# Masked rows in place of 64-row matmuls in attention, and a 16-step blocked scan in the state space layer

## The chip, the cores and the metric

The kernel runs on one core of a Trainium2 chip. The metric is the device time of one execution in microseconds (us). TensorE is PE in the profile, VectorE is DVE, ScalarE is ACT, GpSimd is POOL and SyncE is SP. The queues of SP, ACT and POOL issue the DMAs.

## The reference

Two layers run on a prompt and on eight samples that continue cached sequences. The even layer holds a retention part and a sparse attention with grouped queries: per query block there are compressed keys, selected blocks and a window. The odd layer is a diagonal state space model, and this is its core:

```python
def _s5(u, x0_re, x0_im, lam_re, lam_im, b_re, b_im, c_re, c_im, d, log_step):
    ug = u.reshape(B, L, S5_GROUPS, S5_GROUP)
    dt = jnp.exp(log_step)[:, None]
    mag = jnp.exp(lam_re * dt)
    ang = lam_im * dt
    ab_re, ab_im = mag * jnp.cos(ang), mag * jnp.sin(ang)
...
    bu_re = jnp.einsum('blgc,gpc->blgp', ug, bb_re)
    bu_im = jnp.einsum('blgc,gpc->blgp', ug, bb_im)
    bu_re = bu_re.at[:, 0].add(ab_re * x0_re - ab_im * x0_im)
    bu_im = bu_im.at[:, 0].add(ab_re * x0_im + ab_im * x0_re)
    _, _, xr, xi = lax.associative_scan(_complex_affine_combine, (a_re, a_im, bu_re, bu_im), axis=1)
    y = jnp.einsum('blgp,gcp->blgc', xr, c_re) - jnp.einsum('blgp,gcp->blgc', xi, c_im)
    y = y.reshape(B, L, E) + d * u
    return y, xr[:, -1], xi[:, -1]
```

The state follows x[n+1] = A x[n] + B u[n] with a diagonal complex A, for 64 groups of channels. After it come a gelu and a gated unit with two large matrices.

## The kernel before, in words

The program is written in order, as phases, and a scheduler then fixes one static order of instructions for each engine. Generators are woven: `weave` takes turns among several of them by their stated lengths, so the text of the kernel decides roughly which matmuls stand beside which others.

- Projections and retention (0 to 760 us) come first and are not touched.
- `attention` (783 to 2240) runs 32 units, each a pair of a key group and a query tile. A unit loads its keys (`KA`, `KB`) and queries (`QA`, `QB`). `QB` has 128 rows, the low halves of the split queries and then the high ones; `QA[br]` has the high half in its first 64 rows, and mask rows from 64 on. `scores1` (L1033) computes the compressed scores with two matmuls per head, one on 128 rows (L1039) and one on rows 0 to 63 (L1040). `maxima` (L1122) takes row maxima of the scores before the real pass; its matmuls (L1136) read `kmask` rows, 96 or 64. The loop from L1160 then does the scores (L1182, L1183) and the values (L1171). Projections of the output (L270 to L272) are woven in.
- `sweep_5` (2240 to 2534) normalises the rows and computes the input `u` of the state space layer (L1650 to L1652). Woven with it, `discretise` (L1432) and `tables` (L1333) make powers of A and three kinds of tables: inputs (`wst_s`), outputs (`ca_s`) and responses within a block (`kp_s`). They are written to DRAM.
- `state_space` (L1702) works on blocks of 8 steps. `states_in` multiplies the input tables with blocks of `u` (L1760), two neighbouring blocks being joined with `half`, a product with A to the 8th. `scan` walks 128 steps over all pairs, and 8 more for the samples. `outputs` adds three matmuls per group: the response of the block itself with `T8` (L1846), and the state through `ca` (L1847, L1848), where the second half of the blocks again takes a `half` product.
- A stream `G` of matmuls for the gate (`wz`, L270 to L272 from the end of sweep_5 on) is cut into three parts by `GQ` and woven with the states, the scan and the outputs. For each tile of 24 matmuls POOL does three operations on 128 x 512 elements (L241, L1686). `sweep_E` (2988 to 3584) is the gated unit.

`T8` has two buffers; a refill is eight DMAs, four on SP's queue and four on POOL's (L1826).

Of the kernel before, what the change touches and what calls it, by code (L numbers as in the profile page):

```python
# [18 lines left out]
NT = 16  # L19
# [14 lines left out]
GQ = (80, 220, 40)  # L34
# [86 lines left out]
class K:  # L121
    def __init__(self, tc, a, o, stack, dbg=None):
# [817 lines left out]
    def attention_setup(self, P_, tp):  # L940
# [41 lines left out]
        T.update(KA=KA, KB=KB, VP=VP, tri=tri, triT=triT, idr=idr, cm=cm, cv0=cv0, fk=fk, fa=fa, nd=nd, CKB=CKB, CV=CV, ctx={}, late=[], n_loop=[0], done=set())  # L982

    def attention(self, units, fill, last):
# [30 lines left out]
        def queries(u):  # L1015
# [12 lines left out]
            if t < 4:  # L1028
                nc.vector.memset(QA[0][64:96].bitcast(F32), 0.0)
            nc.vector.tensor_tensor(out=QB[0:64], in0=ps[0:64], in1=QB[0:64], op=OP.subtract)  # L1030
            return QA, QB

        def scores1(u, c):  # L1033
            t, gg = u % NT, u // NT
            QA, QB, CKB = c["QA"], c["QB"], T["CKB"][gg]
# [21 lines left out]
            if t >= 4:  # L1057
# [21 lines left out]
                nc.scalar.copy(out=QA[0][64:96], in_=pb[0:32, 0:1].to_broadcast([32, 4, 128]))  # L1079
# [259 lines left out]
    def tables_in(self, P_):  # L1339
        nc, a, ident, keep = self.nc, self.a, self.ident, self.tc.keep_in_program_order  # L1340
        cp, pp = P_("cpp", 1), P_("ppp", 2, space=PSUM)
        AP = cp.tile([128, 2, 9, 32], F32, name="AP")
# [35 lines left out]
        def inputs(gq):  # L1378

            ab = wk.tile([128, 2, 2, 8, 16], F32, name="ab")  # L1380
            cmul(gq, ab[:, 0], ab[:, 1], BB[0], BB[1], slice(7, None, -1), False)
            return ab

        def store_inputs(gq, ab):

            ps = pp.tile([128, 2, 2, 128], F32, name="pq")
            for j in range(2):
                for i in range(2):
                    nc.tensor.transpose(ps[:, j, i], ab[:, i, j].rearrange("x j c -> x (j c)"), ident)
            ws = wk.tile([128, 2, 2, 2, 64], F32, name="ws")  # L1390
            for j in range(2):
                nc.scalar.copy(out=ws[:, j].rearrange("x r i p -> x i r p"), in_=ps[:, j].rearrange("x i (r p) -> x i r p", r=2))
            nc.sync.dma_start(out=self.wst_s[gq], in_=ws.rearrange("x j r i p -> x (j r i p)"))

        def outputs(gq):

            ca = wk.tile([128, 2, 2, 8, 16], F32, name="ca")
            cmul(gq, ca[:, 0], ca[:, 1], C[0], C[1], slice(1, 9), True)
# [4 lines left out]
        def response(gq, ca):  # L1403

            kp = pp.tile([128, 512], F32, name="pq")[0:32, 0:256].rearrange("x (j n) -> x j n", j=2)
# [5 lines left out]
            kt = wk.tile([32, 2, 128], F32, name="kt")  # L1411
            for j in range(2):
# [7 lines left out]
            nc.scalar.copy(out=kt[:, :, 16:128], in_=kp[:, :, 16:128])  # L1420
            nc.sync.dma_start(out=self.kp_s[gq // 2][64 * (gq % 2):64 * (gq % 2) + 64].rearrange("(j x) n -> x j n", j=2), in_=kt)
# [13 lines left out]
    def discretise(self, P_, pp, AP, BB, C):  # L1435
# [25 lines left out]
        raw = cp.tile([128, 8, 2, 64], F32, name="craw")  # L1461
# [66 lines left out]
        t1, t2 = cp.tile([128, 4, 32], F32, name="pw1"), cp.tile([128, 4, 32], F32, name="pw2")  # L1528
        for m in (1, 2, 4):
            src = AP[:, :, 1:m + 1]  # L1530
            br, bi = [AP[:, i, m].unsqueeze(1).to_broadcast([128, m, 32]) for i in range(2)]
            V.tensor_tensor(out=t1[:, 0:m], in0=src[:, 0], in1=br, op=OP.mult)
            V.tensor_tensor(out=t2[:, 0:m], in0=src[:, 1], in1=bi, op=OP.mult)
            V.tensor_tensor(out=AP[:, 0, m + 1:2 * m + 1], in0=t1[:, 0:m], in1=t2[:, 0:m], op=OP.subtract)
            V.tensor_tensor(out=t1[:, 0:m], in0=src[:, 0], in1=bi, op=OP.mult)
# [449 lines left out]
```

## Time and profile before

| | us |
|---|---|
| median of 3 runs (3555.49 to 3573.8) | 3567.69 |
| the profiled execution | 3586.12 |
| its span | 3584.1 |
| PE, DVE, ACT, POOL busy in the span | 3268.0, 1801.5, 1065.8, 641.6 |
| attention, 783 to 2240 | 1457 |
| sweep_5's rows and the tables, 2285 to 2534.5 | 249.5 |
| states, scan, outputs | 80, 275.8, 97.7 |
| gated unit, 2988 to 3584.1 | 596.1 |

The windows were cut where the first and last instructions of a stage lie. A stage whose engine is busy nearly all the time has that engine as its limit; in the others the reader looks for what is waited for. A matmul's duration overlaps its neighbour's, so what it costs is read from the step between two starts. A matmul of 32-bit numbers that isn't marked as rounded is two records in the trace.

### The profile page before, as it was taken

The page shows a single profiled execution, that of the slowest core. Times are in us where ns is not written, and L with a number is a line of the kernel's source. Part 1 is how long each engine was busy: PE and PEld are TensorE (multiplying, and loading weights), DVE is VectorE, ACT ScalarE, POOL GpSimd, SP SyncE. Part 2 cuts the span into 40 slices and gives each one's busy share as a digit, 9 for nine tenths or more (in the row PEclk, how much of TensorE's full clock was granted, in tenths as well). Part 3 has the DMA queues.
Part 4 walks back from the last instruction along what each step waited for, and adds up shares of the span by engine and source line. Part 5 has one row for each costly group of instructions (what it writes and reads, how often), then busy time and mean ns, then how long its engine had stood idle before and what let it go on. Part 6 is the DMA issues. An engine that isn't in the chain of part 4 may idle for free. (4 is left out here: it accounts for less than half of the span.)

```text
span 3584.1 us, 47826 instructions
## 1 busy us (share of the span) xinstructions
PE 3268.0 (91%) x17425; PEld 2662.5 (74%) x17425; DVE 1801.5 (50%) x4911; ACT 1065.8 (30%) x2312; POOL 641.6 (18%) x729
## 2 busy tenths in 40 slices
PE   7999999979999999979999999799885077999999
PEld 5888778856777778867888888799564065888887
DVE  6455644434555554445545542553799995111222
ACT  4222211113343443433333332442342033111110
POOL 1212221221111110011110000332563062000000
PEclk9999999987898998979999999899998598999999
DMA  5333431133221121222111111554842067222342
GB/s 172 113 119 134 148 76 36 38 90 98 79 76 54 49 75 67 77 70 74 61 63 51 47 42 59 161 177 130 249 153 75 0 190 200 97 71 71 112 136 90
DMA packets 308532, 347.77 MB, mean 97 GB/s; under 512 B 134568, under 2 KB 225256, under 8 KB 306120
## 3 DMA queue, kind: packets, MB, share of 16 engines
q1 hardware_dynamic: 235480, 225.70, 21.5%
q10 hardware_dynamic: 68240, 78.04, 6.4%
q0 software_dynamic: 4576, 40.97, 3.2%
q8 instruction: 138, 2.26, 0.3%
q14 instruction: 98, 0.80, 0.1%
HBM read 231.13 MB, written 117.61 MB: 97 GB/s over the span
## 5 line engine op out<-in xcount | busy, mean ns | idle before, releaser
L1171 PEld LDWEIGHTS ot<-VP,pe 128*128 128x128 f32 x3296 | 446.9, 201 | 37.6 <-issue 9.4
L1171 PE MATMUL ot<-VP,pe 128*128 128x65 f32 x3296 | 438.4, 279 | 0.0
L1187 ACT ACTIVATE pe<-st 128x512 f32<-128x512 f32 x412 | 244.1, 597 | 423.4 <-PE st L1183 327.8
L270 PE MATMUL mm<-we_hi,hT_hi 128*128 128x512 f32 x768 | 304.9, 397 | 0.2 <-ACT hT_hi L226 0.2
L271 PE MATMUL mm<-we_lo,hT_hi 128*128 128x512 f32 x768 | 302.8, 394 | 0.0
L272 PE MATMUL mm<-we_hi,hT_lo 128*128 128x512 f32 x768 | 301.9, 393 | 0.0
L272 PE MATMUL mm<-wz_hi,hT_lo 128*128 128x512 f32 x384 | 155.8, 406 | 144.3 <-POOL hT_lo L241 144.3
L1142 DVE CUSTOM_DVE_ANT_0 tp<-tp,tri 128x256 f32<-128x256 f32 (+3 forms) x352 | 174.5, 504 | 119.3 <-PE tp L1136 110.2
L1136 PE MATMUL tp<-KA,QA 96*128 96x512 f32 (+6 forms) x576 | 209.8, 413 | 0.4 <-DVE mc L1138 0.3
L270 PE MATMUL mm<-we,hT_hi 128*128 128x512 f32 x512 | 201.9, 394 | 5.7 <-ACT hT_hi L240 5.4
L271 PE MATMUL mm<-we,hT_hi 128*128 128x512 f32 x512 | 200.4, 391 | 0.0
L272 PE MATMUL mm<-we,hT_lo 128*128 128x512 f32 x512 | 200.3, 392 | 0.0
L272 PEld LDWEIGHTS mm<-wz_hi,hT_lo 128*128 128x128 f32 x384 | 73.9, 192 | 165.0 <-POOL hT_lo L241 147.6
L1182 PE MATMUL st<-QB,KB 128*128 128x512 f32 x412 | 191.5, 467 | 1.7 <-ACT pe L1187 1.6
L1138 DVE TENSOR_REDUCE mc<-tp 128x1 f32<-128x512 f32 (+2 forms) x196 | 129.9, 672 | 101.1 <-PE tp L1136 99.8
L1157 POOL TENSOR_TENSOR QA<-pms,c_nd 4x512 fp32r<-4x512 f32 x64 | 67.1, 1048 | 620.3 <-ACT pms L1156 606.3
L1183 PE MATMUL st<-QA,KA 100*128 100x512 f32 (+1 forms) x412 | 175.0, 427 | 0.7 <-POOL QA L1157 0.7
L270 PEld LDWEIGHTS mm<-we_hi,hT_hi 128*128 128x128 f32 x768 | 144.7, 188 | 30.4 <-issue 1.0
L272 PEld LDWEIGHTS mm<-we_hi,hT_lo 128*128 128x128 f32 x768 | 144.6, 188 | 30.4 <-issue 0.7
L270 PE MATMUL mm<-wz_hi,hT_hi 128*128 128x512 f32 x384 | 160.4, 418 | 7.0 <-ACT hT_hi L240 7.0
L271 PEld LDWEIGHTS mm<-we_lo,hT_hi 128*128 128x128 f32 x768 | 144.8, 188 | 29.0 <-issue 0.7
L271 PE MATMUL mm<-wz_lo,hT_hi 128*128 128x512 f32 x384 | 157.6, 410 | 0.0
(541 smaller groups left out, 7153.5 us busy)
## 6 DMA issues: line engine op xcount, KB each, us to landing
xT_in<-xT_s SPq DMA_DIRECT2D x48, 512.0 KB
x_in<-x_prompt SPq DMA_DIRECT2D x32, 512.0 KB
xT_s<-xT ACTq DMA_DIRECT2D x32, 512.0 KB
x_in<-x_s SPq DMA_DIRECT2D x32, 512.0 KB
wraw<-w_in_even SPq DMA_DIRECT2D x24, 512.0 KB
qd<-q_s SPq DMA_DIRECT2D x64, 128.0 KB
o_in<-o_s SPq DMA_DIRECT2D x16, 512.0 KB
x_s<-x_in ACTq DMA_DIRECT2D x16, 512.0 KB
```

The source lines that it names most:

```text
L270: nc.tensor.matmul(out=ps[:, 0:n], lhsT=hi[:, k], rhs=whi[:, k], start=k == 0, stop=False)
L271: nc.tensor.matmul(out=ps[:, 0:n], lhsT=hi[:, k], rhs=wlo[:, k], start=False, stop=False)
L272: nc.tensor.matmul(out=ps[:, 0:n], lhsT=lo[:, k], rhs=whi[:, k], start=False, stop=k == 7)
L1136: nc.tensor.matmul(out=pv[:, h], lhsT=qa[0:kmask, h0 + h], rhs=KA[br][0:kmask, (k0 % nt[br]) * 128:(k0 % nt[br] + w) * 128], start=True, s ...
L1138: nc.vector.tensor_reduce(out=mc[:, h0:h0 + hw, i], in_=pv, axis=AX.X, op=OP.max)
L1142: nc.vector.tensor_tensor_reduce(out=pv[:, h], in0=pv[:, h], in1=tri[:, m0:m0 + w].rearrange("p a b -> p (a b)"), scale=1.0, scalar=-3e38, ...
L1157: nc.gpsimd.tensor_tensor(out=qa[r0:r0 + 4], in0=pms.unsqueeze(1).to_broadcast([4, 4, 128]), in1=T["nd"].unsqueeze(2).to_broadcast([4, 4, ...
L1171: nc.tensor.matmul(out=ot[:, h], lhsT=pe[:, 128 * h:128 * h + 128], rhs=VP[br][:, k % nt[br]], start=k == lo and h == 0, stop=k == u and h ...
L1182: nc.tensor.matmul(out=ps, lhsT=KB[br][:, kc], rhs=qb, start=True, stop=False)
L1183: nc.tensor.matmul(out=ps, lhsT=KA[br][0:r0 + 4, kc], rhs=qa[0:r0 + 4].rearrange("p h q -> p (h q)"), start=False, stop=k not in masked)
L1187: nc.scalar.activation(out=pe, in_=ps, func=AF.Exp, scale=0.125)
```

## The change

In attention, `scores1`'s second matmul reads all 128 rows of `QB` against `CKZ`, which holds the high halves of the keys in rows 64 to 127, where `QB` has the high halves of the queries, and zeros in rows 0 to 63. In `maxima` the masks are 96 and 68 rows, and rows 64 to 67 of `QA[1]` are set to zero by POOL for each unit.

In the state space layer the blocks have 16 steps. The tables hold 16 powers for inputs and 17 for A, `u` is stored so that neighbouring blocks lie side by side, and the states come from two accumulating matmuls instead of a product with A to the 8th. Blocks are scanned in eight chains at once: 15 steps over 64 x 8 elements, seven steps that carry the chains' ends over, and 15 corrections of 64 x 7 elements with powers of A. The outputs have a fourth matmul for the off-diagonal half of the block. `T8` now covers two pairs instead of four.

```diff
-GQ = (80, 220, 40)
+GQ = (95, 200, 45)
...
+            nc.gpsimd.memset(CKZ[gg][0:64].bitcast(F32), 0.0)
+            nc.scalar.copy(out=CKZ[gg][64:128], in_=ckd[64:128, gg])
...
+            nc.gpsimd.memset(QA[1][64:68].bitcast(F32), 0.0)
...
                 nc.tensor.matmul(out=ps[:, h, 0:n], lhsT=QB[:, h], rhs=CKB[:, 0:n], start=True, stop=False)
-                nc.tensor.matmul(out=ps[:, h, 0:n], lhsT=QA[0][0:64, h], rhs=CKB[0:64, 0:n], start=False, stop=True)
+                nc.tensor.matmul(out=ps[:, h, 0:n], lhsT=QB[:, h], rhs=CKZ[:, 0:n], start=False, stop=True)
...
-            kmask = 96 if br == 0 and u % NT >= 4 else 64
+            kmask = 96 if br == 0 else 68
...
-            sh = [128, 2, 8, 16]
+            sh = [128, 2, 16, 16]
...
-                    nc.tensor.matmul(out=kp[:, j, 16:128], lhsT=b2[i], rhs=ca[:, i, j, 0:7].rearrange("x k c -> x (k c)"), start=i == 0, stop=i == 1)
+                    nc.tensor.matmul(out=kp[:, j, 16:256], lhsT=b2[i], rhs=ca[:, i, j, 0:15].rearrange("x k c -> x (k c)"), start=i == 0, stop=i == 1)
...
-                        for r in range(2):
-                            nc.tensor.matmul(out=s[:, r, 0:264], lhsT=ws[:, gl % 2, r], rhs=UT[q][:, 2 * gl + r], start=True, stop=True)
...
+                            for r in range(2):
+                                U, o_ = UT[q][:, 4 * (gq % 4) + 2 * j + r], s[:, 2 * j + r]
+                                nc.tensor.matmul(out=o_[:, 0:136], lhsT=ws[:, 1, r], rhs=U[:, 0:136], start=True, stop=False)
+                                nc.tensor.matmul(out=o_[:, 0:128], lhsT=ws[:, 0, r], rhs=U[:, 136:264], start=False, stop=True)
...
+            def step(nx, cur, k, n):
+
+                w = yo.tile([128, 2, 64, 8], F32, name="scan", tag="y2")
+                m = [AT[:, k, i].unsqueeze(2).to_broadcast([128, 64, n]) for i in range(2)]
+                V.tensor_tensor(out=w[:, 0, :, 0:n], in0=cur, in1=m[0], op=OP.mult)
                 for i in range(2):
                     D, O = slice(64 * i, 64 * i + 64), slice(64 - 64 * i, 128 - 64 * i)
-                    V.tensor_tensor(out=w[1][O], in0=x[D], in1=m[1][D], op=OP.mult)
...
+                    V.tensor_tensor(out=w[O, 1, :, 0:n], in0=cur[D], in1=m[1][D], op=OP.mult)
+                for i in range(2):
+                    V.tensor_tensor(out=nx, in0=nx, in1=w[:, i, :, 0:n], op=OP.add)
+
+            def scan():
+
+                for j in range(1, 16):
+                    step(X[:, :, 16 + 8 * j:24 + 8 * j], X[:, :, 8 + 8 * j:16 + 8 * j], 1, 8)
+                    yield
+                for b in range(1, 8):
+                    step(X[:, :, 136 + b:137 + b], X[:, :, 135 + b:136 + b], 16, 1)
+                    yield
+                Y = X[:, :, 9:16]
...
+                for j in range(15):
+                    w = yo.tile([128, 2, 64, 8], F32, name="scan", tag="y2")
+                    for i, x in enumerate((Y, ys)):
+                        V.tensor_tensor(out=w[:, i, :, 0:7], in0=x, in1=AT[:, j + 1, i].unsqueeze(2).to_broadcast([128, 64, 7]), op=OP.mult)
+                    x = X[:, :, 17 + 8 * j:24 + 8 * j]
+                    for i in range(2):
+                        V.tensor_tensor(out=x, in0=x, in1=w[:, i, :, 0:7], op=OP.add)
                     yield
...
+                            T8 = T8s[gp // 2 % 2]
+                            for j in range(8):
+                                (nc.gpsimd if j % 2 else nc.sync).dma_start(out=T8[16 * j:16 * j + 16, :, 16 * j:256], in_=self.kp_s[gp // 2].rearrange("(g c) k -> c g k", c=16)[:, :, 0:256 - 16 * j])
...
-                            nc.tensor.matmul(out=y[:, r, 0:264], lhsT=T8[:, 2 * gl + r], rhs=U, start=True, stop=False)
-                            nc.tensor.matmul(out=y[:, r, 0:136], lhsT=ca[:, r, gl % 2], rhs=X[:, g, 0:136], start=False, stop=False)
-                            nc.tensor.matmul(out=y[:, r, 136:264], lhsT=ca[:, r, gl % 2], rhs=xh[:, r], start=False, stop=True)
...
+                            nc.tensor.matmul(out=y[:, r, 0:264], lhsT=T[:, 0:128], rhs=U, start=True, stop=False)
+                            nc.tensor.matmul(out=y[:, r, 0:128], lhsT=T[:, 128:256], rhs=U[:, 136:264], start=False, stop=False)
+                            nc.tensor.matmul(out=y[:, r, 128:264], lhsT=A[:, 0], rhs=X[:, g, 0:136], start=False, stop=False)
+                            nc.tensor.matmul(out=y[:, r, 0:128], lhsT=A[:, 1], rhs=X[:, g, 8:136], start=False, stop=True)
...
-            weave((scan(), 136), (self.take(G, b_), b_))
+            weave((scan(), 38), (self.take(G, b_), b_))
```

Three places show how the instructions stand. The first is PE in attention, at the end of one unit's compressed scores, before:

```order
L1039 MATMUL tp<-CKB_6687,QB 128x16
L1040 MATMUL tp<-CKB_6687,QA 128x16
L719 MATMUL tp<-c_ident,qn 128x64 x4
L729 MATMUL tp<-c_ident,kn 128x64
L1136 MATMUL tp<-KA_6659,QA 128x128 x2
```

and now (`CKZ` is the new tile, L1140 the line of the maxima):

```order
L1043 MATMUL tp<-CKB_6663,QB 128x16
L1044 MATMUL tp<-CKZ_6665,QB 128x16
L718 MATMUL tp<-c_ident,qn 128x64 x4
L728 MATMUL tp<-c_ident,kn 128x64
L1140 MATMUL tp<-KA_6635,QA 128x128 x2
```

Nothing moved here; the second matmul reads other tiles. The second place is DVE at the end of the scan before, where the first `half` products of the outputs (L1778) come in:

```order
L1789 TENSOR_TENSOR X<-X,scan 128x64
L1784 TENSOR_TENSOR scan<-X,AT_23296 128x64
L1787 TENSOR_TENSOR scan<-X,AT_23296 64x64 x2
L1788 TENSOR_TENSOR X<-X,scan 128x64
L1778 TENSOR_TENSOR h_25874<-X,AT_23296 64x256
L1789 TENSOR_TENSOR X<-X,scan 128x64
```

and DVE now, from the last step over eight chains to the first of the seven that carry their ends:

```order
L1789 TENSOR_TENSOR scan<-X,AT_23421 128x512
L1792 TENSOR_TENSOR scan<-X,AT_23421 64x512 x2
L1794 TENSOR_TENSOR X<-X,scan 128x64x8 x2
L1789 TENSOR_TENSOR scan<-X,AT_23421 128x64
L1792 TENSOR_TENSOR scan<-X,AT_23421 64x64 x2
L1794 TENSOR_TENSOR X<-X,scan 128x64 x2
```

A step still has five operations, of eight times the elements in the first 15. The third place is POOL in the outputs, with `T` the two buffers of `T8`, `yS` the samples' part of the result and `fin` the samples' final states, before:

```order
L1826 DMA T_0_23298<-kp_s_283 16x8x112
L1855 COPY yS<-y_26383 128x4x8
L1775 TENSOR_TENSOR h_26528<-X,AT_23296 128x256
L1813 COPY fin<-XS 128x64
L1775 TENSOR_TENSOR h_26548<-X,AT_23296 128x256
L1826 DMA T_0_23298<-kp_s_283 16x8x80
```

and now:

```order
L1855 DMA T_1_23424<-kp_s_254 16x4x176
L1855 DMA T_1_23424<-kp_s_254 16x4x144
L1859 DMA ca<-ca_s_238 128x2x256
L1855 DMA T_0_23423<-kp_s_255 16x4x240
L1879 COPY yS<-y_25574 128x4x8
L1855 DMA T_0_23423<-kp_s_255 16x4x208
```

The products are gone from POOL, and the refills of the two buffers of `T8` follow each other closely, with the copy of `yS` inside one of them.

## Rows read from the trace of the kernel before

**Rows 1.** The page: PE's busy tenths in 40 slices of 89.6 us.

```profile
PE   7999999979999999979999999799885077999999
```

**Rows 2.** Windows by stage: PE, PEld, DVE, ACT, POOL busy (records), clock, DMA share, GB/s.

```profile
783.00:2240.00 1457.00, 1410.02 (x8015) 1132.74 (x8015) 714.07 (x2433) 532.32 (x1223) 165.56 (x215) 0.91 0.22 68
...
2285.00:2534.50 249.50, 242.37 (x1993) 226.68 (x1991) 104.74 (x288) 95.58 (x219) 98.81 (x112) 0.99 0.57 164
2534.50:2614.50 80.00, 64.49 (x252) 46.43 (x253) 75.09 (x157) 24.95 (x57) 43.72 (x50) 0.98 0.72 227
2614.50:2742.00 127.50, 115.39 (x479) 91.32 (x477) 121.48 (x210) 62.62 (x118) 84.11 (x67) 0.96 0.43 137
2742.00:2890.30 148.30, 11.13 (x37) 8.01 (x37) 134.90 (x477) 3.60 (x7) 11.47 (x12) 0.55 0.02 7
2890.30:2988.00 97.70, 86.61 (x487) 73.69 (x487) 85.10 (x144) 39.20 (x70) 61.57 (x95) 0.97 0.83 240
```

**Rows 3.** Timeline of PE around a 64-row matmul: start us, duration us.

```profile
2122.43 0.40 PE L272 MATMUL acc<-wo_hi,hT_lo 128*128 128x512 f32 x1
2122.75 0.44 PE L1136 MATMUL tp<-KA,QA 64*128 64x384 f32 x1
2123.12 0.50 PE L270 MATMUL acc<-wo_hi,hT_hi 128*128 128x512 f32 x1
2123.46 0.39 PE L271 MATMUL acc<-wo_lo,hT_hi 128*128 128x512 f32 x1
```

**Rows 4.** Timeline of PE around a 96-row matmul.

```profile
2107.29 0.34 PE L1136 MATMUL tp<-KA,QA 96*128 96x384 f32 x1
2107.47 0.40 PE L1182 MATMUL st<-QB,KB 128*128 128x512 f32 x1
2107.70 0.40 PE L1183 MATMUL st<-QA,KA 100*128 100x512 f32 x1
```

**Rows 5.** Groups of weight loads in attention, 64-row maxima alone.

```profile
L1136 PEld LDWEIGHTS tp<-KA,QA 64*128 64x128 f32 x264 | 45.1, 199 | 46.5 <-issue 34.5 <-DVE mc L1142 3.7 <-DVE KB L1011 1.4
```

**Rows 6.** Timeline of PE in one unit's compressed scores.

```profile
1818.57 0.30 PE L1040 MATMUL tp<-CKB,QA 64*128 64x80 f32 x1
1818.80 0.30 PE L1039 MATMUL tp<-CKB,QB 128*128 128x80 f32 x1
```

**Rows 7.** Line L1171 in 1816 to 1818.4: durations ns, first and last start.

```profile
L1171 PEld LDWEIGHTS ot<-VP,pe x16: 189/192/192, 1816.5 to 1818.2; 128*128 128x128 f32 x16
L1171 PE MATMUL ot<-VP,pe x16: 220/275/275, 1816.7 to 1818.3; 128*128 128x65 f32 x16
```

**Rows 8.** Timeline of DVE in sweep_5.

```profile
2400.10 0.41 DVE L1369 TENSOR_TENSOR cm<-C,AP 128x256 f32<-128x256 f32 x1
2400.43 0.68 DVE L1615 TENSOR_TENSOR h_lo<-tp,h_hi 128x512 fp32r<-128x512 f32 x1
2401.03 0.41 DVE L1371 TENSOR_TENSOR cm<-C,AP 128x256 f32<-128x256 f32 x1
```

**Rows 9.** Timeline of DVE in the scan while POOL is idle.

```profile
2799.69 0.27 DVE L1784 TENSOR_TENSOR scan<-X,AT 128x64 f32<-128x64 f32 x1
2801.17 0.27 DVE L1784 TENSOR_TENSOR scan<-X,AT 128x64 f32<-128x64 f32 x1
```

**Rows 10.** Timeline of POOL and DVE in the scan beside the gate stream.

```profile
2640.34 1.29 POOL L241 TENSOR_TENSOR hT_lo<-xT_in,hT_hi 128x512 fp32r<-128x512 f32 x1
2640.50 1.28 DVE L1788 TENSOR_TENSOR X<-X,scan 128x64 f32<-128x64 f32 x1
```

**Rows 11.** Groups of DVE in the same stretch of the scan.

```profile
L1784 DVE TENSOR_TENSOR scan<-X,AT 128x64 f32<-128x64 f32 x40 | 24.2, 605 | 1.4
```

**Rows 12.** Timeline of PE in the outputs.

```profile
2944.16 0.38 PE L1848 MATMUL y<-s,ca 128*128 128x128 f32 x2
2944.38 0.61 PE L1846 MATMUL y<-UT,T 128*128 128x264 f32 x2
```

**Rows 13.** DMA issues in the outputs: KB each, median us to landing.

```profile
T<-kp_s POOLq DMA_DIRECT2D x6, 56.0 KB, 3.9
```

More of the change, by code (lines that the diff above doesn't have):

```diff
@@ L972, in attention_setup @@
         CKB = [cp.tile([128, 128], F32R, name=f"CKB{i}") for i in range(2)]
+        CKZ = [cp.tile([128, 128], F32R, name=f"CKZ{i}") for i in range(2)]
         cv = cp.tile([128, 2, 64], F32, name="CV")
@@ L1527, in discretise @@
         aim = tt(mag, sn, OP.mult, AP[:, 1, 1])
[L1528 to L1535, printed above, removed]
-            V.tensor_tensor(out=t2[:, 0:m], in0=src[:, 1], in1=br, op=OP.mult)
-            V.tensor_tensor(out=AP[:, 1, m + 1:2 * m + 1], in0=t1[:, 0:m], in1=t2[:, 0:m], op=OP.add)
-            yield
@@ L1544, in discretise @@
+        yield from doublings(AP)
+        BP = cp.tile([128, 2, 17, 32], F32, name="BP")
+        keep(V.tensor_copy(out=BP[:, :, 0], in_=AP[:, :, 8]))
+        V.tensor_copy(out=BP[:, :, 1], in_=AP[:, :, 16])
+        yield from doublings(BP)
+        for k in (0, 8, 16):
+            n = min(8, 17 - k)
+            AT = cp.tile([128, 8, 2, 32, 2], F32, name="AT", tag="cw")
             for r in range(2):
@@ L1557, in discretise @@
         fim = tt(tt(tt(aim, lre, OP.mult), tt(nr, lim, OP.mult), OP.subtract), den, OP.mult)
-        w1, w2 = [cp.tile([128, 32, 16], F32, name=f"bw{i}") for i in range(2)]
+        bw = cp.tile([128, 2, 32, 16], F32, name="bw", tag="cw")
+        w1, w2 = bw[:, 0], bw[:, 1]
         fr, fi = [f.unsqueeze(2).to_broadcast([128, 32, 16]) for f in (fre, fim)]
@@ L1750, in states_in @@
                     nc.tensor.transpose(ps[:, 0], raw, ident)
[L1751 removed]
+                    V.tensor_copy(out=UT[q][:, :, 128:136], in_=ps[:, 0].rearrange("x (b g) -> x g b", b=8))
                     yield
[L1753 to L1755 removed]
+                    for gq in range(4 * q, 4 * q + 4):
+                        s = pp.tile([128, 4, 256], F32, name="sp")
+                        for j in range(2):
@@ L1785, in step @@
                 for i in range(2):
                     D, O = slice(64 * i, 64 * i + 64), slice(64 - 64 * i, 128 - 64 * i)
-                    V.tensor_tensor(out=w[O, 1], in0=cur[D], in1=AT[D, j, 1], op=OP.mult)
-                V.tensor_tensor(out=nx, in0=nx, in1=w[:, 0], op=OP.add)
-                V.tensor_tensor(out=nx, in0=nx, in1=w[:, 1], op=OP.add)
-            def scan():
-                for n in range(128):
-                    step(X[:, :, n + 9], X[:, :, n + 8], 1)
+                    V.tensor_scalar(out=ys[O], in0=Y[D], scalar1=-1.0, scalar2=None, op0=OP.mult)
@@ L1794, in scan @@
+                for j in range(15):
[3 more added lines that the diff above has]
+                    x = X[:, :, 17 + 8 * j:24 + 8 * j]
+                    for i in range(2):
+                        V.tensor_tensor(out=x, in0=x, in1=w[:, i, :, 0:7], op=OP.add)
                     yield
-                for b in range(8):
-                    step(XS[:, :, b], X[:, :, b], 0)
-                    yield
+                step(XS, X[:, :, 0:8], 0, 8)
@@ L1823, in outputs @@
                 for q in range(8):
-                    T8 = T8s[q % 2]
-                    for j in range(8):
-                        (nc.gpsimd if j % 2 else nc.sync).dma_start(out=T8[16 * j:16 * j + 16, :, 16 * j:128], in_=self.kp_s[q].rearrange("(g c) k -> c g k", c=16)[:, :, 0:128 - 16 * j])
                     for gl in range(4):
@@ L1840, in outputs @@
-                        w = half(X[:, gs, 8:136], gs)
-                        for i in range(2):
-                            V.tensor_tensor(out=xh, in0=xh, in1=w[i], op=OP.add)
+                            T8 = T8s[gp // 2 % 2]
+                            for j in range(8):
+                                (nc.gpsimd if j % 2 else nc.sync).dma_start(out=T8[16 * j:16 * j + 16, :, 16 * j:256], in_=self.kp_s[gp // 2].rearrange("(g c) k -> c g k", c=16)[:, :, 0:256 - 16 * j])
+                            y2f = yo.tile([128, 4 * 264 + 8], F32, name="y2", tag="y2")
@@ new lines, in outputs @@
+                        yg = y2[:, 2 * (gl % 2):2 * (gl % 2) + 2]
+                        for r in range(2):
+                            o_ = 264 * (2 * (gl % 2) + r)
+                            yh, yi = [v.rearrange("p (h x) -> p h x", h=2)[:, :, 0:128] for v in (y2f[:, o_:o_ + 272], y[:, r, 0:272])]
+                            nc.scalar.activation(out=yh.rearrange("p h (b j) -> p h b j", j=16), in_=yi.rearrange("p h (j b) -> p h b j", b=8), func=AF.Gelu_apprx_tanh)
+                        nc.scalar.activation(out=yg[:, :, 128:136], in_=y[:, :, 128:136], func=AF.Gelu_apprx_tanh)
```

142 lines of the change are left out of this document (66 added, 76 removed).

## Prediction

> **What bounds the kernel now.** I read the 40 slices first: TensorE (PE) is full nearly everywhere, and the one hole, digits 8, 8 and 5 in slices 31 to 33, lies at about 2690 to 2960 us [rows 1]. Then the windows, one for each stage that the change touches [rows 2]. Attention (783 to 2240) has PE busy 1410 of 1457 us: the length of PE's stream is the length of the stage. So has sweep_5 (2285 to 2534.5), 242 of 249.5. In the states (to 2614.5) PE has 64 and VectorE (DVE) 75 of 80 us, so DVE sets the pace. The scan takes 276 us in two parts: 127.5 beside the gate stream, with DVE at 121, and 148 alone, where DVE runs 135 us and PE 11. The outputs (97.7 us) have PE at 87, DVE at 85 and the DMA engines at 0.83, all close together. So attention is to be judged by PE's stream, the scan by DVE's, and the outputs by three things at once.
>
> **Attention: row modes.** Around a lone 64-row matmul the starts are 2122.43, 2122.75, 2123.12, 2123.46: steps of 0.32, 0.37 and 0.34 us [rows 3]. Elsewhere a 512-column matmul on full rows takes a step of 0.23 us (2107.47 to 2107.70), and a 384-column one on 96 rows, between its neighbours on full rows, 0.18 [rows 4]. So the visit costs 0.09 before, 0.19 in itself and 0.11 after, 0.38 in all; 96 rows cost none of it. There are 264 such matmuls in the maxima [rows 5], in 188 unbroken stretches by the order. Neighbours share an entry and an exit, so I take the middle of 0.19 and 0.38, 0.285: 188 x 0.285 = 54 us (ends 36 and 71). With masks of 96 and 68 rows all of these go. In the compressed scores every second matmul has 64 rows; the step is 0.23 although only 80 columns pass [rows 6]. Where matmuls of 65 columns with a new weight each stand in a row on 128 rows, 16 take from 1816.7 to 1818.3, 0.107 each [rows 7]. 32 units x 8 matmuls x 0.123 = 31 us. Together 85 (67 to 102). As PE is idle for 47 us of the stage already, something else ends last at times, and a shorter stream will meet it more often: I take 72. For the unit POOL gets one small memset of 4 x 512 more; POOL is busy for 166 of 1457 us and that hides it; uncovered, 32 of them at the 1.29 us of a full 128 x 512 operation [rows 10] are 41 us at most. The granted clock is 0.91 here and 0.99 in sweep_5 [rows 2]; if half of that gap closed with a fuller stream, 4% of 1410, 56 us more would go, which I don't count. Term: **-72** (0 to -102).
>
> The Trainium skill ("TensorE: Matmul & The Clock Gate", Part 3, "What overlaps and what doesn't") says that weight loads overlap matmuls in flight only where their row groups differ. By that the new scores, all on 128 rows, would pay load and matmul in turn and gain nothing, and the term would be 31 smaller. The trace disagrees: the 16 loads of 192 ns stand beside matmuls that start every 107 ns on the same rows [rows 7].
>
> **Tables and sweep_5.** The tables hold 16 powers instead of 8. PE: 64 matmuls of 240 instead of 112 columns; 128 columns in two passes take 0.22 us, the step from 2944.16 to 2944.38 [rows 12], so 64 x 0.22 = 14; 64 more transposes of 128 columns in one pass, 0.11, are 7. The gate stream's split (95, 200, 45) brings 33 more of its matmuls ahead of the states by the order: 33 x 0.23 = 8. DVE: 192 operations of 512 instead of 256 elements, 0.60 against 0.33 between starts [rows 8], add 51 us to 105 busy of 249.5, so PE's stream covers them, if they come in time. By the order some 70 of the table matmuls now stand behind the last matmul of the rows' sweep, and there little else covers DVE. 14 + 7 + 8 = 29, less the 7 us that PE is idle there, plus some 3 of that tail, where the second set of powers on DVE falls too: **+25** (15 to 45).
>
> **States.** The half products (two DVE operations and one on POOL for each of 32 pairs), two additions and the spill go; two matmuls of 136 and 128 columns replace one of 264, at the same columns. PE's 64 us remain, and DVE has little left: 80 becomes 68, **-12** (-20 to +5, the upper end if the DMA share of 0.72 is what holds it).
>
> **Scan.** Before, 136 steps of five operations on 64 elements, 1.48 us each alone (2799.69 to 2801.17) [rows 9]. After, by the order: 15 steps of five on 512 elements, 7 of five on 64, 15 corrections of four on 448, and one more step that falls beside the outputs. An operation of 64 takes 0.27 and the next starts 0.03 later [rows 9]; one of 512 takes 0.68 [rows 8]. So 75 x 0.71 + 7 x 1.48 + 2 + 60 x 0.65 = 53 + 10 + 2 + 39 = 104.5 us of DVE's own. To that comes POOL. POOL's operation of 2640.34 lasts 1.29 us, and DVE's addition issued 0.16 later takes 1.28 instead of 0.27 [rows 10]: DVE stands still while POOL works. In this stretch 40 steps [rows 11] of 1.48 are 59 us, POOL is busy for 84, and 127.5 pass [rows 2]: 143 less an overlap of 15. The scan keeps 463 of the gate stream's 511 matmuls, so POOL has 84 x 463/511 = 76. 104.5 + 76 - 13 = 168 against 276: **-108**. Ends: no overlap, 181 (-95); no mutual stop at all, about 120, where PE's 463 x 0.23 = 107 and DVE's 104.5 are what is left (-156). I take the first since the row shows the stop on the same two engines and formats.
>
> The Trainium skill ("SBUF — State Buffer", "SBUF: two separate sides") calls it an exclusive lock on the port pair that DVE and GpSimd share, held for a whole instruction. It asks for a DVE operation with two SBUF inputs and a GpSimd operation that reads SBUF, which the wide scan operations and the gate stream still are; by it the stage comes to 168 to 181, and the trace agrees with the 1.28 us.
>
> **Outputs.** Per channel group one matmul of 128 columns more: 64 x 0.22 = 14 us of PE, and 15 more matmuls of the gate stream, 3.5. The half products and the reads of the spill go, so most of DVE's 85 us vanishes. The activation becomes three instructions instead of one, on ScalarE; its 39 busy us of 97.7 hide that, even if they all doubled. Tables are 6.5 instead of 2.4 MB, output coefficients 8.4 instead of 4.2, and 4.2 of spill go: 23.5 MB become 28. At 240 GB/s [rows 2] that is 117 us. T8 is refilled for each two pairs instead of four: four POOL issues, then 3.9 us to landing [rows 13], with a copy that waits for the activation between them. Two buffers make that some 7.3 us per step where 6.1 pass now (97.7/16): 117 us again. **+20** (0 to +35).
>
> **Sum.** -72 + 25 - 12 - 108 + 20 = -147. The profiled execution took 3586.1 us, its span 3584.1 and 2.0 around it; 3439 after. The median of the runs is 18.4 below the profiled one, so 3439 - 18 is about **3420** as a median.
>
> **The rivals.**
> 1. The row modes bring nothing: the waits on DVE, ScalarE and POOL in attention take the place of the visits. For it: PE's stream is woven so that many engines come due at once, and the 47 idle us. Against it: at 714 of 1457 us DVE is far from full. 72 less gain: 3492. 15%.
> 2. The wide operations aren't held up, because their time overlaps POOL's. For it: an overlap of 15 us is there already. Against it: [rows 10]. 48 more gain: 3372. 14%.
> 3. The tables' DVE work bounds sweep_5, since what was 105 us becomes 156 and stands in few places: 15 to 20 us over the term, about 3440 to 3460. 12%.
> 4. Slower than before: the T8 refill becomes a chain of last matmul, issue on POOL behind a waiting copy, landing, first matmul, with no two pairs in flight. It must eat 167 us (147 and the 20 already counted), so each of 16 steps must take 6.1 + 10.4 = 16.5 us; the parts give 2.2 of issue + 3.9 + 6.1 = 12.2 us even fully in turn, 3420 + 80 = 3500. Only if a POOL wait of 4 us comes to each would it tip; then 3570 or more. 3%, and 4% for 3500.
>
> **How the numbers follow.** The forecast has 52%, the rivals 15, 14, 12 and 7. I predict 3420; its own range is 3385 to 3455. The range for 8 in 10 takes in rivals 1 and 3 and most of 2: 3345 to 3495. 0.5% of the time, 18 us, is about what a measurement of this kernel can tell from no change; only rival 4's far end falls outside of faster: faster 0.95, same 0.02, slower 0.03.
>
> **What would show it.** After the change the windows should show: attention about 1385 us with no 64-row matmul and a 128-row step of 0.11 in the scores; states of 68 with DVE mostly idle; a scan of about 168, with wide DVE operations of 0.7 us alone and over 1.3 beside POOL; outputs of about 117 with DMA above 0.8. I am wrong if the attention window shrinks by under 40 us, if wide operations run at 0.7 beside POOL's, or if the outputs show PE waiting for T8's landing on each step.

## The result, and the profile after

The changed kernel takes 3412.47 us (median of 4 runs, 3401.74 to 3436.16), the one before 3561.59 in the same comparisons. The ratio is 0.9587, with a 95% interval of 0.9528 to 0.9646. The forecast was 3420, faster. The profiled execution took 3436.16 us with a span of 3434.4, 149.7 below the span before; by terms the forecast had 147. Both profiled executions lie 24 us above the median of their kernel, so the spans can be compared as well as the medians. The sum came out better than its terms did, as the windows show.

The first view is the page's slices of the changed kernel, to be read against [rows 1]. The hole has narrowed to slice 32, where PE falls to 4 tenths.

```profile
PE   7999999996999999988999998799898497999999
```

The next view is the windows of the changed kernel by stage, cut at the first and last instruction of each, with the columns of [rows 2]: attention, then the rows' sweep, the tail of the tables up to the first states' matmul, the states, the scan, the outputs and the gated unit.

```profile
785.40:2111.90 1326.50, 1275.83 (x7912) 1075.51 (x7912) 700.03 (x2378) 527.01 (x1218) 180.92 (x246) 0.94 0.23 73
...
2169.00:2428.90 259.90, 240.94 (x1934) 223.00 (x1934) 149.47 (x284) 94.18 (x218) 71.98 (x86) 0.96 0.55 160
2428.90:2483.70 54.80, 43.10 (x204) 27.52 (x203) 33.44 (x52) 19.73 (x45) 29.52 (x32) 0.88 0.81 240
2483.70:2554.10 70.40, 61.25 (x379) 53.09 (x378) 3.74 (x18) 22.91 (x42) 22.84 (x19) 0.98 0.84 254
2554.10:2724.50 170.40, 114.61 (x474) 90.53 (x473) 156.68 (x180) 61.02 (x115) 106.58 (x67) 0.83 0.30 103
2724.50:2837.50 113.00, 102.08 (x632) 88.66 (x630) 6.20 (x13) 41.98 (x128) 61.77 (x107) 1.00 0.85 245
2837.50:3434.40 596.90, 570.67 (x2554) 466.19 (x2552) 140.59 (x217) 86.96 (x153) 1.50 (x2) 0.98 0.33 104
```

Cut by the same marks, four stages of the kernel before (attention, rows' sweep, tail, scan):

```profile
782.70:2216.50 1433.80, 1387.90 (x7912) 1115.21 (x7912) 703.48 (x2378) 529.57 (x1218) 164.82 (x214) 0.91 0.22 67
2277.00:2510.10 233.10, 231.57 (x1967) 221.01 (x1967) 102.81 (x277) 87.80 (x204) 84.48 (x93) 0.99 0.53 152
2510.10:2534.60 24.50, 18.62 (x74) 13.21 (x73) 3.32 (x13) 9.20 (x18) 16.85 (x20) 0.92 0.96 274
2614.30:2890.80 276.50, 127.22 (x518) 99.90 (x517) 257.07 (x686) 66.92 (x126) 96.28 (x79) 0.74 0.21 67
```

| stage, us | before | after | difference | forecast |
|---|---|---|---|---|
| attention | 1433.8 | 1326.5 | -107 | -72 |
| from there to the first rows' matmul | 60.5 | 57.1 | -3 | 0 |
| rows' sweep and tail | 257.6 | 314.7 | +57 | +25 |
| states | 79.7 | 70.4 | -9 | -12 |
| scan | 276.5 | 170.4 | -106 | -108 |
| outputs | 96.0 | 113.0 | +17 | +20 |
| gated unit | 597.3 | 596.9 | 0 | 0 |

Three terms are met within 3 us, and two miss by 35 and 32 us with opposite signs. The rows of the changed kernel say what happened in each.

Attention: where every second matmul of the compressed scores had a step of 0.23 [rows 6], all have 0.11 now (PE's timeline, start and duration in us).

```profile
1701.08 0.28 PE L1043 MATMUL tp<-CKB,QB 128*128 128x72 f32 x1
1701.19 0.28 PE L1044 MATMUL tp<-CKZ,QB 128*128 128x72 f32 x1
1701.30 0.28 PE L1043 MATMUL tp<-CKB,QB 128*128 128x72 f32 x1
```

A 384-column matmul of the maxima on 68 rows takes 0.18 between two full ones (2020.26 to 2020.44), as one on 96 rows did [rows 4]; the entry and exit of [rows 3] are gone.

```profile
2020.03 0.40 PE L271 MATMUL acc<-wo_hi,hT_lo 128*128 128x512 f32 x1
2020.26 0.34 PE L1140 MATMUL tp<-KA,QA 68*128 68x384 f32 x1
2020.44 0.40 PE L269 MATMUL acc<-wo_hi,hT_hi 128*128 128x512 f32 x1
```

Rows' sweep: the tile that takes the powers for the scan to DRAM has one buffer, which later products use too. In the timeline of the changed kernel DVE waits for its stores three times, 10.7 us in all (the number in brackets is the idle time before, with what ended it; `bw` is the first later product in that buffer), the row norm's small operation (L209) stands behind that on DVE, POOL's scaling behind it, and PE's transposes come last, 13.21 us late.

```profile
2182.56 0.29 DVE L1561 COPY AT<-BP 64x256 f32<-64x256 f32 x1 [5.48 <-DMA at_s<-AT]
...
2188.13 0.17 DVE L1561 COPY AT<-BP 64x32 f32<-64x32 f32 x1 [3.56 <-DMA at_s<-AT]
...
2190.87 0.69 DVE L1575 TENSOR_TENSOR bw<-B,t 128x512 f32<-128x512 f32 x1 [1.64 <-DMA at_s<-AT]
...
2194.86 0.14 DVE L209 TENSOR_SCALAR n_v<-n_ss 128x1 f32<-128x1 f32 x1
...
2195.80 2.86 POOL L1614 TENSOR_SCALAR x_in<-x_in,n_r 128x1024 f32<-128x1024 f32 x1
2198.71 1.54 PE L1626 MATMUL tp<-c_ident,x_in 128*128 128x128 f32 x6 [13.21 <-POOL x_in L1614]
```

Scan: DVE and POOL take turns. Of the next rows the first is four POOL operations in one, and the others are wide operations on DVE that stand beside them.

```profile
2594.94 6.77 POOL L195 TENSOR_TENSOR wz_lo<-wraw,wz_hi 128x512 fp32r<-128x512 f32 x4
...
2595.57 1.66 DVE L1789 TENSOR_TENSOR scan<-X,AT 128x512 f32<-128x512 f32 x1
2597.26 3.32 DVE L1792 TENSOR_TENSOR scan<-X,AT 64x512 f32<-64x512 f32 x2
2600.61 1.64 DVE L1794 TENSOR_TENSOR X<-X,scan 128x512 f32<-128x512 f32 x1
```

An operation of 0.68 us [rows 8] takes 1.64 to 1.67 here, as 0.27 became 1.28 in [rows 10]. When POOL has nothing to do, the corrections start every 0.54 us:

```profile
2689.47 0.61 DVE L1813 TENSOR_TENSOR scan<-X,AT 128x448 f32<-128x448 f32 x1
2690.01 0.61 DVE L1816 TENSOR_TENSOR X<-X,scan 128x448 f32<-128x448 f32 x1
```

POOL has nothing to do there because a load of output coefficients (`ca`) waits on SP's queue for a buffer that the scan's sign-changed copy (`ys`) holds, and the gate stream's row loads stand behind it. SP issues the load at 2710.46, and ScalarE and PE go on with the gate stream after 50.77 and 43.65 idle us:

```profile
2710.46 0.52 SPq L1859 DMA_DIRECT2D ca<-ca_s  x1
...
2715.14 0.62 ACT L239 CAST hT_hi<-xT_in 128x512 fp32r<-128x512 f32 x1 [50.77 <-DMA xT_in<-xT_s]
...
2716.79 0.79 PE L269 MATMUL mm<-wz_hi,hT_hi 128*128 128x512 f32 x1 [43.65 <-ACT zr L1700]
```

Outputs: the second half of one channel group and the first of the next, without the gate stream between them, take from 2731.62 to 2732.74, 1.12 us for what took 0.90 before (0.45 for L1846, then 0.23 and 0.22 [rows 12]). The new matmul is L1865.

```profile
2731.62 0.61 PE L1864 MATMUL y<-UT,T 128*128 128x264 f32 x2
2732.06 0.38 PE L1865 MATMUL y<-UT,T 128*128 128x128 f32 x2
2732.28 0.40 PE L1866 MATMUL y<-X,ca 128*128 128x136 f32 x2
2732.52 0.38 PE L1867 MATMUL y<-X,ca 128*128 128x128 f32 x2
2732.74 0.61 PE L1864 MATMUL y<-UT,T 128*128 128x264 f32 x2
```

### The profile page after: what moved, and what is told of

Same layout as the page of the kernel before. It is cut to its first block, busy times and chain, and to the rows that moved or that the text cites. A ratio compares the mean times of both kernels' runs of the same rounds, so it can differ in the third digit from the quotient of the medians.

```text
span 3434.4 us, 47838 instructions
## 1 busy us (share of the span) xinstructions
PE 3190.7 (93%) x17745; PEld 2652.5 (77%) x17745; DVE 1621.4 (47%) x4172; ACT 1077.6 (31%) x2394; POOL 647.5 (19%) x739
## 4 chain that ended last, share of the span: by engine, by line
PE 70%; DVE 8%; DMA 4%; ACT 1%; issue 1%; SPq 1%; POOL 1%; ACTq 0%; DVEq 0%; POOLq 0%
PE ot L1175 11%; PE mm L269 7%; PE mm L270 7%; PE mm L271 7%; PE tp L1140 4%; PE st L1186 3%; PE st L1187 3%; PE acc L269 2%; PE acc L753 2%; PE acc L271 2%; PE acc L270 2%; PE mm L1667 2%; PE mm L1665 2%; PE mm L1666 2%; DVE scan L1792 1%; PE acc L910 1%
## 5 line engine op out<-in xcount | busy, mean ns | idle before, releaser
L1175 PEld LDWEIGHTS ot<-VP,pe 128*128 128x128 f32 x3296 | 439.2, 198 | 33.1 <-issue 5.6
L1175 PE MATMUL ot<-VP,pe 128*128 128x65 f32 x3296 | 427.9, 275 | 0.0
L269 PE MATMUL mm<-wz_hi,hT_hi 128*128 128x512 f32 x384 | 159.0, 414 | 57.8 <-ACT zr L1700 43.6
L1140 PE MATMUL tp<-KA,QA 96*128 96x512 f32 (+6 forms) x576 | 198.5, 394 | 0.7 <-DVE mc L1142 0.3
L1186 PE MATMUL st<-QB,KB 128*128 128x512 f32 x412 | 183.8, 448 | 2.2 <-ACT pe L1191 2.1
L1665 PE MATMUL mm<-h_hi,wu_hi 128*128 128x256 f32 x512 | 148.9, 292 | 3.3 <-ACT uT_out L1670 3.3
```

The source lines that it names most:

```text
L269: nc.tensor.matmul(out=ps[:, 0:n], lhsT=hi[:, k], rhs=whi[:, k], start=k == 0, stop=False)
L1140: nc.tensor.matmul(out=pv[:, h], lhsT=qa[0:kmask, h0 + h], rhs=KA[br][0:kmask, (k0 % nt[br]) * 128:(k0 % nt[br] + w) * 128], start=True, s ...
L1175: nc.tensor.matmul(out=ot[:, h], lhsT=pe[:, 128 * h:128 * h + 128], rhs=VP[br][:, k % nt[br]], start=k == lo and h == 0, stop=k == u and h ...
L1186: nc.tensor.matmul(out=ps, lhsT=KB[br][:, kc], rhs=qb, start=True, stop=False)
L1665: nc.tensor.matmul(out=ps[:, 0:256], lhsT=whi[:, k], rhs=hi[:, k], start=k == 0, stop=False)
```

## The experiments

Medians of different comparisons differ (the kernel before took 3562 us in most, and 3582 in the one with the fifth to eighth experiment), so kernels are compared by their ratios to it, given with 95% intervals, and by stages of their profiles. The changed kernel's ratio is 0.9587.

**Masks alone**, on the kernel before.

```diff
+            nc.gpsimd.memset(QA[1][64:68].bitcast(F32), 0.0)
...
-            kmask = 96 if br == 0 and u % NT >= 4 else 64
+            kmask = 96 if br == 0 else 68
```

> The kernel before with the masks of the maxima alone changed (96 and 68 rows, POOL's memset of four rows). Theory: the visits of 64-row matmuls cost what their steps show, so attention (from the first scores to the last value matmul, 1431 us before) shrinks by 54 us, by up to 75 if the granted clock of 0.91 rises with it; the median is 54 to 75 us below before. Rival: other engines end last without the visits, and less than 25 us are gained.

Measured: 3517.28 us, ratio 0.9862 (0.9813 to 0.9911), which is 49 us less (32 to 67). In the profile attention is 1374.0 us, 60 less:

```profile
783.60:2157.60 1374.00, 1330.68 (x7911) 1110.57 (x7912) 701.50 (x2378) 527.91 (x1218) 180.75 (x246) 0.92 0.22 70
```

I worked out, over all 7911 matmul records of attention, by how much each step exceeds the usual step of the same instruction among full rows at full clock. What falls on changes of row mode was 115 us before and is 61 here: 54 less, as priced. 9 us come from less time at the low clock, the lower of its two levels (1.2 GHz); this much differs between executions of one kernel too, see the next run. Where a step falls under two heads its division is a choice: other choices move these sums by up to 8 us and their differences by up to 5.

**Compressed scores alone**, on the kernel before.

```diff
-                nc.tensor.matmul(out=ps[:, h, 0:n], lhsT=QA[0][0:64, h], rhs=CKB[0:64, 0:n], start=False, stop=True)
+                nc.tensor.matmul(out=ps[:, h, 0:n], lhsT=QB[:, h], rhs=CKZ[:, 0:n], start=False, stop=True)
```

> The kernel before with the compressed scores alone changed (second matmul on 128 rows against zeros). Theory: the eight matmuls of a unit start every 0.11 instead of 0.23 us, 31 us less in attention, up to 40 with the clock. Rival: all on the same 128 rows, each load of weights waits for the matmul before it; the step stays at 0.2 us or more and under 10 us are gained.

Measured: 3506.97 us, ratio 0.9839 (0.9802 to 0.9876), which is 57 us less (44 to 71); in the profile attention is 1349.2, 85 less. Both are more than either theory had:

```profile
783.30:2132.50 1349.20, 1300.23 (x7912) 1055.12 (x7912) 702.06 (x2378) 527.81 (x1218) 164.38 (x214) 0.95 0.23 71
```

By the same accounting, row modes fall from 115 to 82, 32 less, and the time added by the low clock from 88 to 34, 55 less. The granted clock of the stage is 0.95 instead of 0.91. So the mechanism is as priced, and the clock came on top: 55 us between these two profiles, and some 25 by the ratio (57 less 32), since the profile before is one of its kernel's longer executions. That the clock rose with this edit is more than chance: over the whole execution it is 0.945 to 0.949 in all four runs, above each of the 21 that are recorded for the kernel before beside these experiments (0.931 to 0.944), while with the masks alone it stays at 0.932 to 0.943. In the changed kernel with both edits row modes are at 31 (84 less) and the clock's part at 55. How much the clock gives differs between executions: with the same attention code the stage takes 1326 us in the profile of the changed kernel and 1296 to 1319 in nine others below, while its length times its granted clock stays at 1241 to 1243 in the three that I added up (1306 before).

**Tables spread over the rows.** The weave is told a length of 46 turns for the tables. By the code they have 50 now and had 42, so they used to end before the rows and now end after them.

```diff
-            weave((rows, S5[1] - S5[0]), (self.tables(), 33 + 13))
+            weave((rows, S5[1] - S5[0]), (self.tables(), 33 + 21))
```

> The changed kernel, with the tables' length in the weave given as 33+21 instead of 33+13, so that they are spread over the rows' sweep and end with it. Theory: of the 54 us from the last rows' matmul to the first states' matmul (24 before) some 15 to 25 go, since the tables' work on VectorE then lies beside TensorE's rows; the median falls by 10 to 20 us. Rival: the tables' work is a bound wherever it stands; the rows' sweep gets longer by what the tail loses, and the median stays within 6 us.

Measured: 3407.01 us (0.9558, 0.9525 to 0.9590). The windows are the rows' sweep, the tail and the states:

```profile
2142.80:2419.00 276.20, 255.38 (x2030) 231.66 (x2030) 172.47 (x326) 101.36 (x238) 85.41 (x94) 0.96 0.58 167
2419.00:2446.40 27.40, 18.70 (x75) 13.46 (x73) 2.56 (x10) 9.19 (x18) 16.36 (x20) 0.88 0.99 284
2446.40:2524.00 77.60, 70.23 (x412) 61.18 (x413) 3.76 (x18) 26.36 (x49) 27.75 (x22) 0.95 0.77 241
```

The tail falls from 54.8 to 27.4, but the sweep grows from 259.9 to 276.2 and the states from 70.4 to 77.6: 4 us less in all. The rival held. Where the tables stand matters little, what they are costs.

**Two buffers for the powers.**

```diff
-        for k in (0, 8, 16):
-            n = min(8, 17 - k)
-            AT = cp.tile([128, 8, 2, 32, 2], F32, name="AT", tag="cw")
+        for k in (0, 7, 14):
+            n = min(7, 17 - k)
+            AT = cp.tile([128, 7, 2, 32, 2], F32, name="AT", tag="cw" if k == 7 else "at1")
```

> The changed kernel, with the powers for the scan built in three chunks of at most seven in two buffers (one of them apart from the buffer that the later products use), so that VectorE doesn't wait for the chunks' stores (9 to 11 us in all). Theory: that wait holds back the row norm behind it, and TensorE's stall of 13.2 us at 2185 falls to about 4; the median falls by 9 us. Rival: the stall is set by ScalarE, which issues the five stores of the samples' rows (10.9 us) before the row's squares; it stays above 10 us and the median doesn't move.

Measured: 3401.95 us (0.9557, 0.9520 to 0.9594). PE's wait of 13.2 us is 2.5:

```profile
PE tp L1626 <- POOL x_in L1614: 2.5, 1, 2.5
```

The rows' sweep falls from 259.9 to 253.0 us. So the wait is what the trace said, and it is worth some 7 us of the stage, though PE's wait shrank by 11; the medians, 10 us apart, can't tell that from nothing by themselves.

**The gate stream's operations on VectorE.**

```diff
-                hT = self.split_pair(x, P, o["h"], nc.gpsimd)
+                hT = self.split_pair(x, P, o["h"], nc.vector)
...
-                nc.gpsimd.tensor_tensor(out=z[:P], in0=th[:P], in1=z[:P], op=OP.mult)
+                nc.vector.tensor_tensor(out=z[:P], in0=th[:P], in1=z[:P], op=OP.mult)
```

> The changed kernel, with the gate stream's three operations per tile on VectorE instead of POOL. Theory: POOL's operations of 1.29 us stop VectorE for as long as they last, while the same operation takes VectorE 0.69; so the scan falls from 170 to 104.5 + 20 tiles x 3 x 0.69 = 146 us, the states and outputs stay, and the median falls by 20 to 25 us. Rival: the wide operations take 1.6 us for another reason (their strides, or the broadcast factor), and POOL merely runs beside them: then VectorE gets 41 us more to do, the scan goes to about 210 and the median rises by 40.

Measured: 3381.56 us (0.9457, 0.9417 to 0.9497). VectorE has more operations to do and the scan is shorter, 139.8 instead of 170.4 us:

```profile
2517.00:2656.80 139.80, 117.25 (x475) 89.68 (x473) 136.29 (x233) 60.89 (x115) 15.26 (x10) 0.94 0.39 124
```

The median wide operation, which took 1.64 us (L1789) beside POOL, takes 0.68 (durations in ns, least, median, most):

```profile
L1794 DVE TENSOR_TENSOR X<-X,scan x44: 266/687/1761, 2520.2 to 2606.8; 128x512 f32<-128x512 f32 x30, 128x64 f32<-128x64 f32 x14
L1789 DVE TENSOR_TENSOR scan<-X,AT x23: 282/683/1755, 2518.1 to 2654.8; 128x512 f32<-128x512 f32 x16, 128x64 f32<-128x64 f32 x7
```

This settles the scan: it was the turns with POOL that lengthened the wide operations. The eight operations that the edit leaves on POOL there (`wz_lo`) still do it, hence the most of 1761 and 1755. It also bounds VectorE's own part: 55 of the gate stream's operations stand in this window on VectorE, and 136.3 busy less 55 x 0.69 = 38 are 98 us. That is the most it can be, since POOL still holds VectorE up for a part of it; I had 104.5.

**The gate stream out of the scan.**

```diff
-GQ = (95, 200, 45)
+GQ = (95, 1, 244)
```

> The changed kernel, with the gate stream cut 95, 1, 244 instead of 95, 200, 45, so that almost none of it stands in the scan. Theory: the scan is VectorE's own 105 to 110 us (170 in the changed kernel), each wide operation 0.6 to 0.7 us, while the outputs get some 100 us longer and the whole is slower. Rival: the wide operations stay above 1 us without POOL, and the scan stays above 140.

Measured: 3430.3 us in one run. The edit didn't do what it was for: POOL is still busy for 84 us in the scan (106.6 in the changed kernel), and PE still has 357 of 474 matmul records there, so much of the stream stands in the scan whatever the cut says.

```profile
2526.80:2676.50 149.70, 85.25 (x357) 66.76 (x355) 145.61 (x176) 49.46 (x93) 84.21 (x53) 0.79 0.28 93
```

So it can't show the scan alone. It shows that 22 us less of POOL go with 21 us less of scan, and that the outputs become 44 us longer (156.7).

**Response tables loaded twice only.**

```diff
-                            for j in range(8):
+                            for j in range(8 if gp < 4 else 0):
```

> The changed kernel with the response tables T8 loaded for the first two pairs of pairs only and then kept, so that the outputs lack 14 of 16 refills (and use the wrong response for the later groups). Theory: TensorE's stream holds the outputs, with 14 us of added matmuls; they stay at 108 to 113 us. Rival: the refill of the two buffers, or the DMA engines at 0.84, hold them; they fall to 100 us or less.

The kernel leaves out 14 of the 16 refills, so the later groups use a wrong table. Measured: 3397.47 us in one run; the outputs take 101.1 instead of 113.0:

```profile
2698.40:2799.50 101.10, 99.36 (x623) 88.01 (x622) 6.81 (x13) 43.53 (x132) 33.57 (x50) 1.00 0.70 217
```

PE is busy for 99.4 of 101.1 us, where it was busy for 102.1 of 113.0. So the refills held the outputs for 12 us, nearly all of it in PE's waits; the 14 us of the added matmuls stay. My theory, that only PE's stream holds them, was wrong by that; the rival's 100 us was nearer. The edit takes away the wait for a buffer, the issues on POOL (33.6 us busy instead of 61.8) and DMA traffic (0.70 instead of 0.85) at once, and doesn't tell which of them it was.

**Three edits together:** tables' length, two buffers, gate stream on VectorE.

> The changed kernel with three edits together: the tables' length in the weave, the powers for the scan in two buffers, the gate stream's operations on VectorE. Theory: the gains of the parts add up, 4 + 9 + 22 us below the changed kernel, about 3375. Rival: the gate stream's operations on VectorE collide with the tables, which now stand beside them, and no more than the 22 us come.

Measured: 3375.73 us (0.9421, 0.9373 to 0.9469). The ratios of the three parts by themselves would add up to 0.940, inside this interval, but so is the 0.9457 of the gate stream's edit alone, and the ratio doesn't decide. The stages do: from the rows' sweep to the end of the states the profile has 367.9 us, and 378.1 with the gate stream's edit alone, with the same scan (139.8) and outputs (110). Those 10 us are what the other two edits gave by themselves, 4 and 7.

**The gate stream's row loads on ScalarE's queue**, on the changed kernel.

```diff
-                nc.sync.dma_start(out=x[:, :, 0:P], in_=self.xT_s[t])
+                nc.scalar.dma_start(out=x[:, :, 0:P], in_=self.xT_s[t])
```

> The changed kernel, with the gate stream's row loads (xT_in) on ScalarE's queue instead of SP's. In the changed kernel SP issues nothing from before 2655 to 2710.46, when the last reader of the scan's sign-changed copy (ys) frees the buffer for a load of output coefficients (ca); the row loads stand behind that load, and TensorE waits 43.6 us for the gate stream. Theory: on another queue the loads aren't held up, the stall falls below 10 us, some 100 of the gate stream's matmuls run beside the corrections, and the median falls by 8 to 15 us. Rival: POOL then works beside the corrections and holds up VectorE by as much as TensorE gains; the stall goes, but the median stays within 5 us.

Measured: 3413.03 us (0.9582, 0.9519 to 0.9645), no gain. The wait of 43.6 us is gone, and PE now waits for the scan itself:

```profile
PE y L1866 <- DVE X L1816: 29.9, 1, 29.9
PE mm L269 <- ACT hT_hi L239: 13.0, 2, 12.8
```

The rival held in its result: PE was early, and VectorE is what ends last. More time lost to POOL, the rival's reason, isn't seen: VectorE is busy for 157.3 us in the scan, as before the edit (156.7).

**The last two** add the row loads on POOL's queue to the three edits, the second also with the gate stream cut 80, 240, 25.

> The three edits together (tables' length, powers in two buffers, gate stream's operations on VectorE), and the gate stream's row loads on POOL's queue, which now has little else to do in the scan. Theory: 3376 becomes 3365 or less, since the gate stream isn't held up behind the load of output coefficients. Rival: with VectorE as the bound of the scan at 137 of 140 us nothing comes free, and the time stays at 3370 to 3380.

Measured: 3369.24 us (0.9450, 0.9392 to 0.9509), between the theory and the rival, and its ratio can't be told from that of the three edits.

> The same four edits, and the gate stream cut 80, 240, 25. Theory: 4 more of its tiles (23 us of TensorE, 8 us of VectorE) stand in the scan, where TensorE has room, and leave states and outputs, which TensorE holds: 10 to 15 us less than the run with 95, 200, 45. Rival: states and outputs are held by the DMA engines at 0.80 to 0.87 and don't get shorter, the scan gets 8 us longer, and the time is the same or higher.

Measured: 3385.04 us (0.9515, 0.9443 to 0.9587). States, scan and outputs:

```profile
2446.10:2513.70 67.60, 56.72 (x357) 49.08 (x357) 11.76 (x31) 20.17 (x37) 2.13 (x4) 0.97 0.72 225
2513.70:2674.10 160.40, 136.77 (x570) 106.91 (x569) 149.72 (x252) 73.10 (x139) 25.36 (x31) 0.94 0.39 129
2674.10:2791.30 117.20, 95.93 (x574) 84.04 (x573) 9.85 (x18) 35.96 (x117) 46.18 (x95) 0.94 0.76 221
```

In the run before it these were 71.0, 141.1 and 115.3. The scan grows by 19 us, the states lose 3 and the outputs nothing, with PE at 96 of 117 us there: the rival held.

## Why the prediction was right, and where it wasn't

The time, 3412 against 3420, is right, and so is the likeliest case with its direction. That it came so close is partly luck, since attention gained 35 us more than its term and the sweep lost 32 more. Of the terms:

- **Attention** was mis-sized by the clock. The price of the row modes, 85 us, is what the accounting finds (84; 54 and 32 alone). The 13 us taken off it for other engines that come due are the size of what small steps and waits grew by, 13 us, though PE's idle time in the windows grew by only 5 (45.9 to 50.7), so that the reason isn't shown. That makes 71 against 72. What failed is counting nothing for the clock, which the text named with up to 56 us: the low clock added 88 us before and 55 after, 33 less. The Trainium skill's rule on weight loads ("TensorE: Matmul & The Clock Gate", Part 3, "What overlaps and what doesn't") was rightly put aside: the step of 0.11 stands on the same 128 rows.
- **Tables and sweep** were mis-sized too, by 32 us. The accounting finds 28 us more of PE's own work, which the step had (29). What failed are the waits: the term took 7 us of idle PE as filled and put 3 for the tail, but waits grew by 25 us in the sweep and the tail (idle PE in the windows: 30.7 us, 7.4 before), and some 4 more are the lower clock. 11 of the 25 are PE's wait for the powers' store, which is a wait added by a shared buffer and which I didn't look for in the diff. The longer tail looks like the rival of the tables' work, but VectorE is busy for only 183 of the 315 us, and spreading the tables moved the tail and didn't remove it; that rival stays undecided. Its time, 3440 to 3460, doesn't follow from its own 15 to 20 us either, which make 3435 to 3440.
- **States** as forecast; the upper end with the DMA engines (0.84) didn't come.
- **Scan** right, and partly by luck. VectorE's own part is at most 98 and not 104.5: the 60 operations of the corrections don't wait for each other and start every 0.54 us, not 0.65. POOL was busy for 107 and not 76, since its operations get longer too (1.73 where they take 1.27 alone). From VectorE's last step at 2714 to the first state matmul of the outputs at 2724.5 PE catches up with the gate stream.
- **Outputs** right in size. PE's busy time grew by 17 us, the matmuls, and its idle time stayed at 11. Most of the idle time comes from the refills now, 9 us by the seventh run; before it was the wait for the half products, which are gone (below). So the refills cost the stage 12 us, but not by the 7.3 us per step of the forecast, which isn't worked out from its parts.
- **Rivals:** row modes without effect, no mutual stop, and the chain of refills that eats the whole gain are refuted by the first two, the fifth and the seventh run.

PE's wait in the outputs before:

```profile
PE y L1848 <- DVE s L1842: 10.7, 9, 2.1
```

What stays open: why the granted clock in attention differs between executions of the same code, and why the scores' edit raised it and the masks' did not; and how the rest of the sweep's waits, some 15 us, divide.

## What to carry to other kernels

Price a stage by the steps between starts, at full clock, and treat the clock as a term of its own with its own range: here it was 33 of the 107 us of the stage. When a change makes a table larger, look in the diff for tiles that now share a buffer, since a store that must land first is a wait on an engine that has others queued behind it. And where two engines take turns, count an operation of the slower one as a loss on the faster one before you put it there: 55 operations moved from POOL to VectorE shortened the scan by 30 us.

## What the runs showed of the hardware that was not expected

A POOL operation and a wide VectorE operation that fall together take 1.69 us as a pair (6.77 for four), and both are recorded longer than alone. Alone, VectorE's start every 0.60 us [rows 8] and POOL's every 1.23:

```profile
2717.34 1.28 POOL L1702 TENSOR_TENSOR zr<-th,zr 128x512 f32<-128x512 f32 x1 [0.18 <-ACT th L1701]
2718.57 2.53 POOL L240 TENSOR_TENSOR hT_lo<-xT_in,hT_hi 128x512 fp32r<-128x512 f32 x2
```

By these starts the pair is 1.83 in sum, by the recorded durations 1.95. That each is stretched is what a lock that each waits for would give. But a lock held for the whole of either instruction, as the Trainium skill ("SBUF — State Buffer", "SBUF: two separate sides") has it, would make the pair last the sum, and it lasts some 0.14 us less by the starts: the two exclude each other for most of their time, not for all of it. Which part is free isn't shown.

On 68 rows a matmul costs no more than on 96 or 128, so the price of [rows 3] is one of leaving full rows for 64, not of using fewer than 128.
